# Transposes of attention weights, values and gate inputs moved from TensorE to the DMA engines as 16-bit planes

## The chip, the cores and the metric

The kernel runs on one core of a Trainium2 chip. A core has a matrix engine (TensorE, PE in the profile, with its weight loads as PEld), a vector engine (VectorE, DVE), an activation engine (ScalarE, ACT), a general engine (GpSimd, POOL) and a queue engine (SyncE, SP). Each runs its own list of instructions strictly in order and waits on semaphores; 16 DMA engines move data between the device memory and the on-chip memory (SBUF). TensorE writes to a second on-chip memory (PSUM). The metric is the device time in microseconds of one execution, as a median over runs.

## The reference, cut to what matters

One layer of an encoder is applied to 256 prompt positions and 64 sample positions (320 columns, `T`), model width 2048:

```python
xn = rmsnorm(x, norm_mix)
q, k, v, u, vs, g = split(xn @ w_in)
a  = stick_breaking(q, k, v)             # 8 heads of 128; the sample also sees 256 cached keys
u  = gelu(u);  vs = rmsnorm(gelu(vs), sgu_norm)
bb = spatial_gate(u, vs)                 # per group: s = w_spatial @ vs over 128 positions, then u * s
merged = g_a * (a @ w_branch_a) + g_b * (bb @ w_branch_b)
h = x + merged @ w_out
h = h + (silu(gate) * up) @ w_down       # gate, up = rmsnorm(h) @ w_gate_up
y = rmsnorm(h)
```

Everything is 32-bit floating point. The stick-breaking weights `w` of a head are a matrix of queries by keys. The step after it, `w @ v`, and the spatial gate both sum over positions, so TensorE needs positions on the partitions: the weights, the values `v` and the normalised `vs` have to be transposed on the way.

## The kernel before, in words

All activations are kept with features on the 128 partitions and the 320 positions along the row. Every dense product is made of blocks: `block()` (line 88 on) loads 1024 columns of weights (512 KB) with one DMA of SP into a buffer `raw` (3 buffers), ScalarE rounds them to `wh` (line 75), VectorE takes the remainder `wl = raw - wh` (line 76; 4 buffers of each), and TensorE does 8 x 3 products of 128 by 320 (lines 83, 84, 85). After each such block the counter `tick()` goes up by one; `at(tick, fn)` puts a piece of side work at a later tick. The blocks are numbered here from 0, from the first block after the first two heads; block 0 is the first of the `k` projection of head 2.

The order on each engine is fixed when the program is built: a scheduler places instructions by dependences and priorities, and DMAs wrapped in `keep_in_program_order` keep their mutual order. At run time an engine that waits holds everything that stands behind it.

Attention goes by pairs of heads, 0 to 3. `att_scores` makes scores `z`, ScalarE and VectorE turn them into weights (absolute value, exponential, logarithm, a running sum, exponential) in `z[0]` (128x640), `z[1]` (128x384 used) and `wown` (128x128). `att_turn` then transposes 14 blocks of 128x128 on TensorE with the identity matrix: 4 of `v` (line 383), 1 of `vo`, the sample's part of `v` which GpSimd collects (384), 6 of `z` (387), 2 of `z[0]` (389) and `wown` (390). The results lie in PSUM; ScalarE and VectorE copy them to `av` and `wt` (lines 393 to 397). `att_out` multiplies them (403) and splits the result into `B` (117, 118, 416, 417). In the spatial gate, `sgu_gain` scales `vs`, `sgu_turn` transposes 5 blocks for each of 4 pairs of groups (490, 491) and ScalarE copies them out (494, 495), and `sgu_mix` multiplies (503, 505).

Of the kernel before, what the change touches and what calls it, by code (L numbers as in the profile page):

```python
# [8 lines left out]
F32 = mybir.dt.float32  # L9
# [4 lines left out]
P = 128  # L14
TP = 256
TS = 64
T = TP + TS
D = 2048
KD = D // P
H = 8  # L20
# [13 lines left out]
def stream_step(ctx: ExitStack, tc: tile.TileContext, xT, w_in, w_a, w_b, w_out, w_gu, w_down,  # L34
                gains, ws_t, bs, ck_t, cv, y_t, k_t, v_t, sv_t):
    nc = tc.nc
# [65 lines left out]
    def pair(name):  # L102
        return big.tile([P, 2 * T], F32, tag="D", bufs=8, name=name)
# [36 lines left out]
    ident = const.tile([P, P], F32, name="ident")  # L140
# [142 lines left out]
    attn = {}  # L283
    att_ctx = ExitStack()
    apool = att_ctx.enter_context(tc.tile_pool(name="attn", bufs=1))
# [21 lines left out]
    Z, KT = 384, T + PAST  # L307
# [13 lines left out]
    def att_new(p):  # L321
        attn[p] = {"q": apool.tile([P, 2, T], F32, tag="q", bufs=2, name="q"),
                   "k": apool.tile([P, 2, KT], F32, tag="k", bufs=2, name="k"),
                   "v": apool.tile([P, 2, T], F32, tag="v", bufs=2, name="v"),
                   "vo": apool.tile([P, P], F32, tag="vo", name="vo")}

    def att_keys(p):
        tc.keep_in_program_order(nc.sync.dma_start(
# [44 lines left out]
        for r in ROWS:  # L373
            nc.scalar.activation(out=wown[r, r], in_=z[1][r, Z:], func=AF.Exp)

    def att_turn(p):

        s = attn[p]
        z, v = s["z"], s["v"]
        ba, bb, bs_, bv = aux(), aux(), aux(), aux()  # L380
        cols = lambda t, i: t[:, i * P : (i + 1) * P]
        for i in range(4):
            nc.tensor.transpose(cols(bv, i), v[:, i // 2, i % 2 * P : (i % 2 + 1) * P], ident)  # L383
        nc.tensor.transpose(cols(ba, 3), s["vo"], ident)
        for j, b in enumerate((ba, bb)):
            for i in range(3):
                nc.tensor.transpose(cols(b, i), cols(z[j], i), ident)  # L387
        for i in range(2):
            nc.tensor.transpose(cols(bs_, i), cols(z[0], 3 + i), ident)
        nc.tensor.transpose(cols(bs_, 2), wown, ident)  # L390
        wt = s["wt"] = apool.tile([P, 3 * Z], F32, tag="wt", name="wt")
        av = s["av"] = apool.tile([P, 5 * P], F32, tag="av", name="av")
        nc.scalar.copy(out=av[:, 0 : 4 * P], in_=bv)
        nc.vector.tensor_copy(wt[:, 0:Z], ba[:, 0:Z])
        nc.vector.tensor_copy(av[:, 4 * P :], ba[:, Z:])
        nc.scalar.copy(out=wt[:, Z : 2 * Z], in_=bb[:, 0:Z])
        nc.scalar.copy(out=wt[:, 2 * Z :], in_=bs_[:, 0:Z])

    def att_out(p):
        s = attn.pop(p)  # L400
        wt, av, cvt = s["wt"], s["av"], s["cv"]
        po = aux1(), aux()
        mm = lambda out, a, b, first, last: nc.tensor.matmul(out, a, b, start=first, stop=last, skip_group_check=True)  # L403

        mm(po[0][:, TP : TP + P], av[:, 4 * P :], wt[:, 2 * Z + 2 * P :], True, False)
        for j, r in enumerate(ROWS):
            for i in range(2):
                lo = 2 * Z + i * P + j * TS
                mm(po[0][:, TP + j * TS : TP + (j + 1) * TS], cvt[:, i, j, :], wt[:, lo : lo + TS], False, i == 1)
        for j in range(2):  # L410
            mm(po[j][:, 0:TP], av[:, 2 * j * P : (2 * j + 1) * P], wt[:, j * Z : j * Z + TP], True, False)
            mm(po[j][:, P:TP], av[:, (2 * j + 1) * P : (2 * j + 2) * P], wt[:, j * Z + TP : (j + 1) * Z], False, True)
# [8 lines left out]
    def head_out(name, ps, h):  # L421
        s = attn[h // 2]
        o = s[name][:, h % 2, 0:T]
        if name == "q":
            nc.vector.scalar_tensor_tensor(out=o, in0=ps, scalar=QSCALE, in1=got["rx"],
                                           op0=ALU.mult, op1=ALU.mult)
        else:
            nc.vector.tensor_tensor(out=o, in0=ps, in1=got["rx"], op=ALU.mult)
            nc.gpsimd.dma_start(out=(k_t if name == "k" else v_t)[h], in_=o)
        if name == "v":  # L430
            nc.gpsimd.tensor_copy(s["vo"][:, ROWS[h % 2]], o[:, TP:T])

    def first_out():
        for name, b in (("q", 0), ("k", 1), ("v", 2)):
# [33 lines left out]

    us, _ = halves(H, "us")
    bT: dict[int, tuple] = {}  # L470
    vown, vnat = {}, {}

    def sgu_norm():
        got["rv"] = rms("rv", [sq.total], H * P)
        sgu_gain(0)

    def sgu_gain(p):

        own = vown[p] = apool.tile([P, 2, T], F32, tag="q", bufs=2, name="vown")[:, 0, 0:P]
        for j in range(2):  # L480
            g = 2 * p + j
            for out, r in ((vs[g][:, 0:TP], slice(0, TP)), (own[:, j * TS : (j + 1) * TS], slice(TP, T))):
                nc.vector.scalar_tensor_tensor(out=out, in0=vs[g][:, r], scalar=g_sgu[:, g : g + 1],
                                               in1=got["rv"][:, r], op0=ALU.mult, op1=ALU.mult)
            nc.gpsimd.dma_start(out=sv_t[g], in_=own[:, j * TS : (j + 1) * TS])

    def sgu_turn(p):
        pt, po = aux(), aux()
        for i in range(4):
            nc.tensor.transpose(pt[:, i * P : (i + 1) * P], vs[2 * p + i // 2][:, i % 2 * P : (i % 2 + 1) * P], ident)  # L490
        nc.tensor.transpose(po[:, 0:P], vown.pop(p), ident)
        t = apool.tile([P, 5 * P], F32, tag="av", name="vsn") if p % 2 else apool.tile([P, 3 * Z], F32, tag="wt", name="vsn")
        vn = vnat[p] = t[:, 0 : 5 * P].rearrange("p (i d) -> p i d", i=5)
        nc.scalar.copy(out=vn[:, 0:4].rearrange("p i d -> p (i d)"), in_=pt)
        nc.scalar.copy(out=vn[:, 4], in_=po[:, 0:P])
        if p + 1 < H // 2:
            sgu_gain(p + 1)
# [20 lines left out]
    def sgu_both(p):  # L518
        if p:
            sgu_mix(p - 1)  # L520
        if p < H // 2:
            sgu_turn(p)
# [14 lines left out]
    for m in range(KD):  # L537
        gate = []
        for i in range(2):
            ps = block(w_in[5 * H + i * KD + m], xs)  # L540
            t = t320("ev")
# [8 lines left out]
        t = t320("mg", 1)  # L550
# [5 lines left out]
        lo = mpool.tile([P, T], F32R, tag="C", bufs=32, name="ml")  # L556
# [72 lines left out]
    ms, r = (const.tile([P, 3], F32, name=f"col{i}") for i in range(2))  # L629
# [9 lines left out]
    for n in (1, 1, 2, 2, 2, 2, 2, 2, 1, 1):  # L639
        y = ypair[done // 2].rearrange("p (c t) -> p c t", c=2)[:, done % 2 : done % 2 + n, :]  # L640
# [57 lines left out]
```

## Time and profile before

| | |
|---|---|
| Median of 3 runs | 1716.69 us (1716.69 to 1718.19) |
| The profiled execution | 1716.78 us |
| Its span, first to last instruction | 1715.0 us |
| TensorE busy | 1702.2 us, 99% |
| VectorE, ScalarE, GpSimd busy | 861.9, 658.8, 46.1 us |
| Mean rate of the DMA engines | 154 GB/s |
| Attention and spatial gate, from its first scores to the last mix | about 63 to 327 us |

A row of the page or of a view gives, for a group of instructions, the source line, the engine, the operation, what it writes and reads, the shape, the count, the busy time in us, the mean of one in ns, and the idle time of the engine just ahead of them with what ended it. A timeline row gives start, duration, engine, line. Matmuls overlap in the pipeline, so a matmul's duration is longer than the distance to the next one; the distance is what it costs.

### The profile page before, as it was taken

The numbers are of one execution on the slowest core, as the hardware profiler recorded it, in microseconds if no ns is written. First come the engines' busy times: TensorE is split into PE (matmuls) and PEld (weight loads), VectorE is DVE, ScalarE is ACT, GpSimd is POOL, SyncE is SP. The second block draws the span as 40 slices with busy tenths as digits, with TensorE's granted clock in tenths as the row PEclk, the third lists the DMA queues.
The fourth block names the chain that finished last, engine by engine and source line by source line (L and its number), as shares of the span: only waits on it lengthen the run. The fifth ranks groups of instructions, "written<-read, shape, count | busy, mean of one in ns | idle before, by whom it ended". The sixth has DMA issues, their size and how long they took to land.

```text
span 1715.0 us, 27450 instructions
## 1 busy us (share of the span) xinstructions
PE 1702.2 (99%) x11616; PEld 1696.7 (99%) x11616; DVE 861.9 (50%) x1097; ACT 658.8 (38%) x819; POOL 46.1 (3%) x73
## 2 busy tenths in 40 slices
PE   9999999999999999999999999999999999999997
PEld 9999999999999999999999999999999999999997
DVE  7655446544444445555444444444444444444454
ACT  6454454433333333444333332233333323333332
POOL 0100011000000000110000000000000000000000
PEclk9999999999999999999999999999999999999999
DMA  7554444444444445554444445444444444444453
GB/s 260 162 193 143 144 154 145 139 148 148 149 153 152 148 152 165 174 171 149 150 148 148 150 152 153 148 148 148 152 151 152 148 148 150 151 153 149 130 150 114
DMA packets 80331, 263.32 MB, mean 154 GB/s; under 512 B 9008, under 2 KB 15408, under 8 KB 80208
## 3 DMA queue, kind: packets, MB, share of 16 engines
q1 hardware_dynamic: 78704, 258.25, 46.6%
q0 software_dynamic: 1088, 3.02, 0.5%
q8 instruction: 91, 1.49, 0.3%
q10 hardware_dynamic: 416, 0.31, 0.1%
q14 instruction: 32, 0.26, 0.0%
HBM read 256.03 MB, written 5.51 MB: 152 GB/s over the span
## 4 chain that ended last, share of the span: by engine, by line
issue 54%; PE 45%; DVE 0%; DMA 0%; ACT 0%; POOL 0%; POOLq 0%; ACTq 0%; DVEq 0%
PE acc L83 13%; PE acc L84 13%; PE acc L85 13%; PE aux L219 2%; PE acc L219 1%; PE aux L403 1%; DVE h L637 0%; DMA raw<-w_in 0%; PE aux L505 0%; PE aux L343 0%; PE aux L345 0%; PE aux L387 0%; PE aux L342 0%; PE aux L490 0%; PE aux L383 0%
## 5 line engine op out<-in xcount | busy, mean ns | idle before, releaser
L75 ACT CAST wh<-raw 128x1024 fp32r<-128x1024 f32 x468 | 484.5, 1036 | 988.0 <-PE acc L84 796.3
L76 DVE TENSOR_TENSOR wl<-raw,wh 128x1024 fp32r<-128x1024 f32 x468 | 564.2, 1206 | 506.4 <-ACT wh L75 503.9
L83 PE MATMUL acc<-A,wh 128*128 128x320 f32 x2464 | 763.1, 310 | 0.0
L85 PE MATMUL acc<-A,wl 128*128 128x320 f32 x2464 | 761.5, 309 | 0.0
L84 PE MATMUL acc<-A,wh 128*128 128x320 f32 x2464 | 761.4, 309 | 0.0
L83 PEld LDWEIGHTS acc<-A,wh 128*128 128x128 f32 x2464 | 462.6, 188 | 2.1 <-issue 2.0
L84 PEld LDWEIGHTS acc<-A,wh 128*128 128x128 f32 x2464 | 462.6, 188 | 0.2
L85 PEld LDWEIGHTS acc<-A,wl 128*128 128x128 f32 x2464 | 462.6, 188 | 0.0
L85 PE MATMUL acc<-B,wl 128*128 128x320 f32 x960 | 296.6, 309 | 0.0
L83 PE MATMUL acc<-B,wh 128*128 128x320 f32 x960 | 296.6, 309 | 0.0
L84 PE MATMUL acc<-B,wh 128*128 128x320 f32 x960 | 296.6, 309 | 0.0
L83 PEld LDWEIGHTS acc<-B,wh 128*128 128x128 f32 x960 | 180.2, 188 | 0.0
L84 PEld LDWEIGHTS acc<-B,wh 128*128 128x128 f32 x960 | 180.2, 188 | 0.0
L85 PEld LDWEIGHTS acc<-B,wl 128*128 128x128 f32 x960 | 180.2, 188 | 0.0
L83 PE MATMUL acc<-mh,wh 128*128 128x320 f32 x256 | 79.1, 309 | 0.0
L84 PE MATMUL acc<-ml,wh 128*128 128x320 f32 x256 | 79.1, 309 | 0.0
L85 PE MATMUL acc<-mh,wl 128*128 128x320 f32 x256 | 79.1, 309 | 0.0
L597 DVE TENSOR_TENSOR bb<-acc,rh 128x320 f32<-128x320 f32 x44 | 21.6, 491 | 57.8 <-PE acc L85 57.8
L594 DVE TENSOR_TENSOR ev<-acc,rh 128x320 f32<-128x320 f32 x44 | 21.6, 491 | 56.4 <-PE acc L85 56.3
L83 PEld LDWEIGHTS acc<-mh,wh 128*128 128x128 f32 x256 | 48.0, 188 | 0.0
L84 PEld LDWEIGHTS acc<-ml,wh 128*128 128x128 f32 x256 | 48.0, 188 | 0.0
L85 PEld LDWEIGHTS acc<-mh,wl 128*128 128x128 f32 x256 | 48.0, 188 | 0.0
(173 smaller groups left out, 696.2 us busy)
## 6 DMA issues: line engine op xcount, KB each, us to landing
raw<-w_gu SPq DMA_DIRECT2D x176, 512.0 KB, 3.5
raw<-w_in SPq DMA_DIRECT2D x141, 512.0 KB, 3.6
raw<-w_down SPq DMA_DIRECT2D x80, 512.0 KB, 3.5
raw<-w_out SPq DMA_DIRECT2D x32, 512.0 KB, 3.6
raw<-w_a SPq DMA_DIRECT2D x16, 512.0 KB, 3.5
raw<-w_b SPq DMA_DIRECT2D x16, 512.0 KB, 3.5
raw<-w_down SPq DMA_DIRECT2D x16, 256.0 KB, 2.7
xr<-xT SPq DMA_DIRECT2D x16, 160.0 KB, 2.6
```

What stands on the lines that cost most here:

```text
L75: nc.scalar.copy(out=wh[:, : n * P], in_=raw[:, : n * P])
L76: nc.vector.tensor_tensor(out=wl[:, : n * P], in0=raw[:, : n * P], in1=wh[:, : n * P].bitcast(F32), op=ALU.subtract)
L83: nc.tensor.matmul(ps[:, :T], a, x[0], start=first, stop=False)
L84: nc.tensor.matmul(ps[:, :T], a, x[1], start=False, stop=False)
L85: nc.tensor.matmul(ps[:, :T], b, x[0], start=False, stop=last)
L219: nc.tensor.matmul(first[b][h][:, :T], w[:, (h * n + j) * P : (h * n + j + 1) * P], xs[c + j][i], start=not last and c + j + i == 0, stop= ...
L403: mm = lambda out, a, b, first, last: nc.tensor.matmul(out, a, b, start=first, stop=last, skip_group_check=True)
L594: nc.vector.tensor_tensor(out=t, in0=pg, in1=got["rh"], op=ALU.mult)
L597: nc.vector.tensor_tensor(out=u, in0=pu, in1=got["rh"], op=ALU.mult)
```

## The change

The 76 transposes on TensorE go. In their place `apart` has ScalarE copy a 32-bit tile into two planes of 16-bit halves, one behind the other in a row (read with a stride, written straight). `turn` has SP issue one DMA that transposes all 128x128 blocks of both planes (a 128x1280 tile of 16-bit words is 10 blocks, 320 KB; the `wp1` tile is 128x1024, 8 blocks, 256 KB). `together` has VectorE copy the two planes back into every second half-word of a 32-bit tile. The planes and the turned planes are 128x640 tiles of the pool with 8 buffers that also holds `z`, `vs` and `us`. For a pair of heads there are three DMA transposes (`vp`, `wp0`, `wp1`), for a pair of groups one (`vsp`): 16 in all. GpSimd's copy to `vo` goes. The ticks of the side work change: the output of a pair of heads comes 16 ticks after its start instead of 14.

```diff
+    def planes(name, n):
+        return pair(name)[:, 0:n].bitcast(U16).rearrange("p (w n) -> p w n", w=2)
+    def apart(to, src):
+        nc.scalar.copy(out=to, in_=src.bitcast(U16).rearrange("p (n w) -> p w n", w=2))
+    def turn(src):
+        to = planes("turned", src.shape[2])
+        flat = lambda t: t.rearrange("p w n -> p (w n)")
+        tc.keep_in_program_order(nc.sync.dma_start(
+            out=flat(to).rearrange("p (b r) -> p b r", r=P), in_=flat(src), transpose=True))
+        return to
+    def together(to, src):
+        nc.vector.tensor_copy(to.bitcast(U16).rearrange("p (n w) -> p w n", w=2), src)
...
+        y = s["wp"] = planes("wp0", 5 * P), planes("wp1", 4 * P)
+        apart(y[0], z[0])
+        apart(y[1][:, :, 0:Z], z[1][:, 0:Z])
+        apart(y[1][:, :, Z:], wown)
-    def att_turn(p):
...
-        for i in range(4):
-            nc.tensor.transpose(cols(bv, i), v[:, i // 2, i % 2 * P : (i % 2 + 1) * P], ident)
-        nc.tensor.transpose(cols(ba, 3), s["vo"], ident)
-        for j, b in enumerate((ba, bb)):
-            for i in range(3):
-                nc.tensor.transpose(cols(b, i), cols(z[j], i), ident)
-        for i in range(2):
-            nc.tensor.transpose(cols(bs_, i), cols(z[0], 3 + i), ident)
-        nc.tensor.transpose(cols(bs_, 2), wown, ident)
...
-        nc.scalar.copy(out=av[:, 0 : 4 * P], in_=bv)
-        nc.vector.tensor_copy(wt[:, 0:Z], ba[:, 0:Z])
-        nc.vector.tensor_copy(av[:, 4 * P :], ba[:, Z:])
-        nc.scalar.copy(out=wt[:, Z : 2 * Z], in_=bb[:, 0:Z])
-        nc.scalar.copy(out=wt[:, 2 * Z :], in_=bs_[:, 0:Z])
+    def att_turn(p, what):
         s = attn[p]
+        s[what] = [turn(t) for t in ((s["vp"],) if what == "vt" else s["wp"])]
+    def att_join(p, what):
...
+            together(av, t[0])
...
+            together(wt[:, 0 : 5 * P], t[0])
+            together(wt[:, 5 * P :], t[1])
...
         if name == "v":
-            nc.gpsimd.tensor_copy(s["vo"][:, ROWS[h % 2]], o[:, TP:T])
...
+            apart(s["vp"][:, :, j * TP : (j + 1) * TP], o[:, 0:TP])
+            apart(s["vp"][:, :, 4 * P + j * TS : 4 * P + (j + 1) * TS], o[:, TP:T])
...
         at(now + 2, att_scores, p)
-        at(now + 4, att_rows, p)
-        at(now + 10, att_turn, p)
-        at(now + 14, att_out, p)
+        at(now + 6, att_turn, p, "vt")
+        at(now + 11, att_rows, p)
+        at(now + 8, att_join, p, "vt")
+        at(now + 12, att_turn, p, "wt")
+        at(now + 14, att_join, p, "wt")
+        at(now + 16, att_out, p)
...
     def sgu_turn(p):
...
-        for i in range(4):
-            nc.tensor.transpose(pt[:, i * P : (i + 1) * P], vs[2 * p + i // 2][:, i % 2 * P : (i % 2 + 1) * P], ident)
-        nc.tensor.transpose(po[:, 0:P], vown.pop(p), ident)
...
-        nc.scalar.copy(out=vn[:, 0:4].rearrange("p i d -> p (i d)"), in_=pt)
-        nc.scalar.copy(out=vn[:, 4], in_=po[:, 0:P])
+        vturned[p] = turn(vplane.pop(p))
+    def sgu_join(p):
...
+        together(t[:, 0 : 5 * P], vturned.pop(p))
...
-    for p in range(H // 2 + 1):
-        at(base + 4 * p + 2 + (p == 0), sgu_both, p)
+    for p, mix in enumerate((9, 11, 14, 18)):
+        at(base + 1 + 3 * p, sgu_gain, p)
+        at(base + 6 + 3 * p, sgu_turn, p)
+        at(base + (8, 10, 13, 16)[p], sgu_join, p)
+        at(base + mix, sgu_mix, p)
```

More of the change, by code (lines that the diff above doesn't have):

```diff
@@ L323, in att_new @@
                    "k": apool.tile([P, 2, KT], F32, tag="k", bufs=2, name="k"),
-                   "v": apool.tile([P, 2, T], F32, tag="v", bufs=2, name="v"),
-                   "vo": apool.tile([P, P], F32, tag="vo", name="vo")}
+                   "v": apool.tile([P, 2, T], F32, tag="v", bufs=2, name="v")}
+    U16 = mybir.dt.uint16
+    def planes(name, n):
[10 more added lines that the diff above has]
+        nc.vector.tensor_copy(to.bitcast(U16).rearrange("p (n w) -> p w n", w=2), src)
     def att_keys(p):
@@ L374, in att_scores @@
             nc.scalar.activation(out=wown[r, r], in_=z[1][r, Z:], func=AF.Exp)
-    def att_turn(p):
-        s = attn[p]
-        z, v = s["z"], s["v"]
-        ba, bb, bs_, bv = aux(), aux(), aux(), aux()
-        cols = lambda t, i: t[:, i * P : (i + 1) * P]
-        for i in range(4):
-            nc.tensor.transpose(cols(bv, i), v[:, i // 2, i % 2 * P : (i % 2 + 1) * P], ident)
-        nc.tensor.transpose(cols(ba, 3), s["vo"], ident)
-        for j, b in enumerate((ba, bb)):
-            for i in range(3):
-                nc.tensor.transpose(cols(b, i), cols(z[j], i), ident)
-        for i in range(2):
[L389 to L394, printed above, removed]
-        nc.vector.tensor_copy(av[:, 4 * P :], ba[:, Z:])
-        nc.scalar.copy(out=wt[:, Z : 2 * Z], in_=bb[:, 0:Z])
-        nc.scalar.copy(out=wt[:, 2 * Z :], in_=bs_[:, 0:Z])
+        y = s["wp"] = planes("wp0", 5 * P), planes("wp1", 4 * P)
[3 more added lines that the diff above has]
+    def att_turn(p, what):
+        s = attn[p]
+        s[what] = [turn(t) for t in ((s["vp"],) if what == "vt" else s["wp"])]
+    def att_join(p, what):
+        s = attn[p]
+        t = s[what]
+        if what == "vt":
+            av = s["av"] = apool.tile([P, 5 * P], F32, tag="av", name="av")
+            together(av, t[0])
+        else:
+            wt = s["wt"] = apool.tile([P, 9 * P], F32, tag="wt", name="wt")
+            together(wt[:, 0 : 5 * P], t[0])
+            together(wt[:, 5 * P :], t[1])
     def att_out(p):
@@ L403, in att_out @@
         mm = lambda out, a, b, first, last: nc.tensor.matmul(out, a, b, start=first, stop=last, skip_group_check=True)
-        mm(po[0][:, TP : TP + P], av[:, 4 * P :], wt[:, 2 * Z + 2 * P :], True, False)
+        mm(po[0][:, TP : TP + P], av[:, 4 * P :], wt[:, 8 * P :], True, False)
         for j, r in enumerate(ROWS):
             for i in range(2):
-                lo = 2 * Z + i * P + j * TS
+                lo = Z + i * P + j * TS
                 mm(po[0][:, TP + j * TS : TP + (j + 1) * TS], cvt[:, i, j, :], wt[:, lo : lo + TS], False, i == 1)
         for j in range(2):
-            mm(po[j][:, 0:TP], av[:, 2 * j * P : (2 * j + 1) * P], wt[:, j * Z : j * Z + TP], True, False)
-            mm(po[j][:, P:TP], av[:, (2 * j + 1) * P : (2 * j + 2) * P], wt[:, j * Z + TP : (j + 1) * Z], False, True)
+            w = wt[:, j * 5 * P : j * 5 * P + Z]
+            mm(po[j][:, 0:TP], av[:, 2 * j * P : (2 * j + 1) * P], w[:, 0:TP], True, False)
+            mm(po[j][:, P:TP], av[:, (2 * j + 1) * P : (2 * j + 2) * P], w[:, TP:], False, True)
         aT[2 * p] = split("B", po[0][:, 0:T])
@@ L430, in head_out @@
         if name == "v":
-            nc.gpsimd.tensor_copy(s["vo"][:, ROWS[h % 2]], o[:, TP:T])
+            j = h % 2
+            if j == 0:
+                s["vp"] = planes("vp", 5 * P)
+            apart(s["vp"][:, :, j * TP : (j + 1) * TP], o[:, 0:TP])
+            apart(s["vp"][:, :, 4 * P + j * TS : 4 * P + (j + 1) * TS], o[:, TP:T])
     def first_out():
@@ L470, in stream_step @@
     bT: dict[int, tuple] = {}
-    vown, vnat = {}, {}
+    vplane, vturned, vnat = {}, {}, {}
     def sgu_norm():
         got["rv"] = rms("rv", [sq.total], H * P)
-        sgu_gain(0)
     def sgu_gain(p):
-        own = vown[p] = apool.tile([P, 2, T], F32, tag="q", bufs=2, name="vown")[:, 0, 0:P]
+        own = apool.tile([P, 2, T], F32, tag="q", bufs=2, name="vown")[:, 0, 0:P]
         for j in range(2):
@@ L485, in sgu_gain @@
             nc.gpsimd.dma_start(out=sv_t[g], in_=own[:, j * TS : (j + 1) * TS])
+        y = vplane[p] = planes("vsp", 5 * P)
+        for j in range(2):
+            apart(y[:, :, j * TP : (j + 1) * TP], vs[2 * p + j][:, 0:TP])
+        apart(y[:, :, 4 * P :], own)
     def sgu_turn(p):
-        pt, po = aux(), aux()
-        for i in range(4):
[L490 to L493, printed above, removed]
-        nc.scalar.copy(out=vn[:, 0:4].rearrange("p i d -> p (i d)"), in_=pt)
-        nc.scalar.copy(out=vn[:, 4], in_=po[:, 0:P])
-        if p + 1 < H // 2:
-            sgu_gain(p + 1)
+        vturned[p] = turn(vplane.pop(p))
+    def sgu_join(p):
+        t = apool.tile([P, 5 * P], F32, tag="av", name="vsn") if p % 2 else apool.tile([P, 9 * P], F32, tag="wt", name="vsn")
+        together(t[:, 0 : 5 * P], vturned.pop(p))
+        vnat[p] = t[:, 0 : 5 * P].rearrange("p (i d) -> p i d", i=5)
     def sgu_mix(p):
@@ L516, in sgu_mix @@
             bT[g] = split("B", b)
[L518 to L522, printed above, removed]
     base = state["tick"]
     at(base + 1, sgu_norm)
-    for p in range(H // 2 + 1):
-        at(base + 4 * p + 2 + (p == 0), sgu_both, p)
+    for p, mix in enumerate((9, 11, 14, 18)):
[3 more added lines that the diff above has]
+        at(base + mix, sgu_mix, p)
     for g in range(H):
```

## The prediction

> **What bounds the kernel now.** I read the page first: busy times, then TensorE's row in the 40 slices and the granted clock.
>
> ```profile
> PE 1702.2 (99%) x11616; PEld 1696.7 (99%) x11616; DVE 861.9 (50%) x1097; ACT 658.8 (38%) x819; POOL 46.1 (3%) x73
> PE   9999999999999999999999999999999999999997
> PEclk9999999999999999999999999999999999999999
> ```
>
> TensorE works in every slice at full clock; the others are half idle. So what leaves TensorE shortens the time, as long as nothing makes TensorE wait. Who waits for whom is the second view, the grouped instructions with the idle time ahead of them:
>
> ```profile
> L75 ACT CAST wh<-raw 128x1024 fp32r<-128x1024 f32 x452 | 474.5, 1050 | 973.1 <-PE acc L84 781.4 <-issue 161.1 <-DMA raw<-w_in 17.9
> L76 DVE TENSOR_TENSOR wl<-raw,wh 128x1024 fp32r<-128x1024 f32 x452 | 553.2, 1225 | 506.3 <-ACT wh L75 503.9 <-PE acc L219 2.3
> ```
>
> ScalarE's rounding waits for TensorE (781 us in all), that is for a free `wh` buffer. The weights run ahead. How far, the third view tells, the timeline, here of VectorE and TensorE at block 8:
>
> ```profile
> 77.90 3.49 DVE L76 TENSOR_TENSOR wl<-raw,wh 128x1024 fp32r<-128x1024 f32 x3
> 78.66 0.31 PE L83 MATMUL acc<-A,wh 128*128 128x320 f32 x1
> 78.80 0.31 PE L84 MATMUL acc<-A,wh 128*128 128x320 f32 x1
> 79.39 0.31 PE L85 MATMUL acc<-A,wl 128*128 128x320 f32 x1
> ```
>
> Five products from 78.66 to 79.39 are 0.147 us apart, so a block of 24 takes 3.52 us. In steady running a `wl` is ready some 8 us before it is used (4 buffers: three blocks, 10.6 us, less 1.05 and 1.22 for rounding and remainder). But each `att_scores` takes ScalarE and VectorE for some 12 us, and the lead shrinks: the first of the three remainders in that row, block 8's, ends at 79.1 and is used at 79.39.
>
> **The change part by part.** *Transposes removed.* The chain of work that ended last gives TensorE's pace in them, the groups their count.
>
> ```profile
> 135.22 0.66 PE aux L387 x6
> 311.32 0.44 PE aux L490 x4
> ```
> ```profile
> L387 PE MATMUL aux<-ident,z 128*128 128x128 f32 x24 | 3.3, 272 | 0.0
> L490 PE MATMUL aux<-ident,vs 128*128 128x128 f32 x16 | 2.6, 272 | 0.0
> L383 PE MATMUL aux<-ident,v 128*128 128x128 f32 x16 | 2.4, 272 | 0.0
> L389 PE MATMUL aux<-ident,z 128*128 128x128 f32 x8 | 1.5, 272 | 0.0
> L491 PE MATMUL aux<-ident,vown 128*128 128x128 f32 x4 | 1.1, 273 | 0.0
> L384 PE MATMUL aux<-ident,vo 128*128 128x128 f32 x4 | 1.1, 273 | 0.0
> L390 PE MATMUL aux<-ident,wown 128*128 128x128 f32 x4 | 1.1, 272 | 0.0
> ```
>
> 24+16+16+8+4+4+4 = 76 transposes, each 272 ns long but 0.66/6 = 0.11 us apart: 8.3 us on the path. All other products stay. This is the whole gain there can be: -8.3 us.
>
> *ScalarE.*
>
> ```profile
> L75 ACT CAST wh<-raw 128x512 fp32r<-128x512 f32 x16 | 9.9, 622 | 14.9 <-PE acc L84 14.9
> L393 ACT COPY av<-aux 128x512 f32<-128x512 f32 x4 | 2.3, 578 | 0.0
> L397 ACT COPY wt<-aux 128x384 f32<-128x384 f32 x4 | 2.0, 492 | 0.0
> ```
>
> Its price per column comes from its casts of 1024 and of 512: (1050-622)/512 = 0.84 ns, plus 194 ns. For a pair of heads: `v` 2 x (0.62+0.30), `z[0]` 1.26 (1280 half-words), `z[1]` 0.84, `wown` 0.41, together 4.4 us; away go 0.58 and two of 0.49. A pair of groups gets 1.65 us, and loses a 0.59 and a short one. In all it is about +14 us.
>
> ```profile
> core 0: us, PE busy (x) PEld busy (x) DVE busy (x) ACT busy (x) POOL busy (x), PEclk, DMA share, GB/s
> 60.00:252.00 192.00, 192.00 (x1320) 188.06 (x1319) 103.06 (x156) 97.78 (x137) 16.22 (x24) 1.00 0.48 157
> ```
>
> In the attention alone ScalarE is idle for 94 us and VectorE for 89. Where they matter is order: the 2.5 us of `wp0` and `wp1` stand ahead of roundings 11, 20 and 32, just where the lead is thin. At 11 ScalarE waits for a DMA anyway (3 us); at 20 and 32 they cost 1 to 2 us of lead.
>
> *VectorE.* A join writes 1280 or 1024 half-words with a stride. The nearest rows are its copies from PSUM:
>
> ```profile
> L394 DVE COPY wt<-aux 128x384 f32<-128x384 f32 x4 | 2.2, 550 | 0.0
> L350 DVE COPY z<-aux 128x128 f32<-128x128 f32 x8 | 2.2, 279 | 0.0
> ```
>
> At (550-279)/256 = 1.06 ns per column a join takes 1.5 or 1.2 us, perhaps half; 16 joins, 23 us, against 3.3 us of copies that go. I take 1.5. VectorE has the room, but in its list the joins stand between remainders: the `v` join ahead of blocks 12, 22, 33 and 44, the `wt` joins ahead of 13 and 14, of 23 (both), of 35 (both), of 50 and 51. **A join waits for a DMA, and behind it wait the remainders that TensorE needs.** That is the one dangerous place. GpSimd's eight copies to `vo`, off the path, go.
>
> *SP and the DMA queues.* 16 transposing DMAs, and the one of `cv` is moved. No row shows a transposing DMA. What is near:
>
> ```profile
> raw<-w_in SPq DMA_DIRECT2D x141, 512.0 KB, 3.6
> y_t<-h SPq DMA_DIRECT2D x6, 320.0 KB, 2.3
> k<-ck_t SPq DMA_DIRECT2D x4, 256.0 KB, 4.6
> sv_t<-vown POOLq DMA_DIRECT2D x8, 32.0 KB, 2.0
> ```
>
> The lower end is a copy at the rate that the queues reach in a burst, some 250 GB/s: 1.3 us of queue time for 320 KB. The upper end is the slowest row with lines of 256 bytes, like those of a 128x128 block of half-words: 32 KB in 2.0 us, ten blocks one after the other, 20 us. I take 2 us of queue time and about 5 us to landing, near the rows of 320 and 256 KB. The Trainium skill (DMA: Bandwidth & Descriptors, section on latency and other measured facts) gives 261 GB/s for a transposing DMA; by it 320 KB are 1.3 us, no stall arises below, and the sum would be 1708.5 us. No run here shows it yet.
>
> *What this does to the lead.* Two stretches after scores (the last two columns are the DMA engines' share and GB/s), then SP, ScalarE and TensorE in the second of them:
>
> ```profile
> 79.10:90.20 11.10, 11.10 (x78) 11.10 (x77) 6.67 (x8) 3.98 (x5) 1.06 (x2) 1.00 0.78 267
> 117.70:127.60 9.90, 9.90 (x69) 9.90 (x68) 5.27 (x6) 2.41 (x3) 0.54 (x1) 1.00 0.78 249
> ```
> ```profile
> 117.69 1.60 SPq L70 DMA_DIRECT2D raw<-w_in  x2
> 120.06 10.26 SPq L70 DMA_DIRECT2D raw<-w_in  x4
> ```
> ```profile
> 127.65 1.05 ACT L75 CAST wh<-raw 128x1024 fp32r<-128x1024 f32 x1 [1.48 <-PE acc L85]
> ```
> ```profile
> 139.85 0.31 PE L85 MATMUL acc<-A,wl 128*128 128x320 f32 x1
> ```
>
> There three loads go out almost at once, as the `raw` buffers were held, and the DMA engines are at 78%. Into that burst SP's new list puts, for pair 1: load 21, `vp`, load 22, `cv`, the keys, load 23, `wp0`, `wp1`. Load 23, landed by 127.6 before, and then both transposes carry 896 KB + 256 KB more. At 249 GB/s that is 4.7 us; the burst starts 1.1 us sooner (the `B` splits of pair 0 no longer stand in it), so `wp1` lands at about 131.2. Joins and remainder 23 end at 134.2. The use is at 139.85 less pair 1's own 14 transposes, 1.5 us: 138.3. Margin 4 us. For pair 2:
>
> ```profile
> 169.34 16.28 SPq L70 DMA_DIRECT2D raw<-w_in  x6
> 188.24 0.31 PE L85 MATMUL acc<-A,wl 128*128 128x320 f32 x1
> ```
>
> Pair 2 has the same order. There `wp0`, `wp1` and the splits push rounding 32, so load 35 goes out at about 172.8 instead of 169.3, the transposes land near 179.5, and joins and remainder 35 end at 183.4; it is used at 188.3-1.5 = 186.8. Margin 3 us. Pair 0:
>
> ```profile
> 88.72 1.22 DVE L76 TENSOR_TENSOR wl<-raw,wh 128x1024 fp32r<-128x1024 f32 x1
> ```
> ```profile
> 98.51 0.31 PE L85 MATMUL acc<-A,wl 128*128 128x320 f32 x1
> ```
>
> Pair 0 is tighter. Remainder 13 ends at 89.9 and is used at 98.5-1.5 = 97.0; 4.4 us of transfers and 1.5 of a join leave 1 to 1.5 us. Pair 3's `wp0` comes behind load 51, out of the burst, and the gate's four behind loads 61, 63, 67 and 71. By the same reckoning both have some 7 us to spare beyond a landing in 5 us. At my 2 us per 320 KB the three bursts get 1.9 us more than at the copy rate: pair 0 stalls by 0.5, the others not. I add 0.7 for what SP loses in issuing. Sum: 1716.78 - 8.3 + 1.2 = 1709.7 us for the profiled execution (span 1715.0, 1.8 outside it), which lies 0.1 above the median.
>
> **The rivals.** *Slower transposes.* The mechanism is the join that holds VectorE. With queue time r times a copy's, a burst takes (r-1) x 3.7 us more; what exceeds margins of 1.3, 4 and 3 is stall. At r = 2.5 that is 4.3+1.6+2.6 = 8.5 us: from there the kernel is slower. At r = 4: 9.8+7.1+8.1 = 25, 1733 us. For it: small lines (the 32 KB row runs at 16 GB/s). Against: 256 KB beside loads in 4.6 us. *About even.* r from 2.2 to 2.8, stalls of 5 to 11 us: 1713 to 1720. *Block after block.* Ten blocks at 2.0 us each: 28 blocks in a burst take 56 us, three bursts stall by about 50 each, pair 3 by 20, the gate by 40: about 1920. Only a fixed price per block would do it, and that 2.0 us is mostly one latency, so I hold it unlikely. The Trainium skill (VectorE: DVE Perf Modes, section on the three transpose paths) has 1309 ns for one 128x128 block by DMA against 390 on TensorE; multiplied by ten, its figure is an estimate of 1815 us on the same reckoning. *The change does not do what it says:* only if TensorE did not go straight on to the next block; its row has no gap, so I give that nothing.
>
> **How the numbers follow.** Forecast 0.57 (stall below 5 us, 1708.5 to 1713), even 0.12, slower transposes 0.23, block after block 0.08. A difference under 0.2%, 3.4 us, can't be told from none. Faster: 0.57; same 0.12; slower 0.31. The likeliest own range is 1708 to 1713; the range for all is 1707.5 (the whole gain and a little of the runs' scatter) to 1733 (r = 4), with about 0.1 above it.
>
> **What would show it.** Right: no transposes on TensorE, 8.3 us fewer in the chain, DMA rows of `turned` landing within 5 us, TensorE waiting for `wl` by 2 us at most, near blocks 12 to 14. Wrong: VectorE's joins (line 344) waiting for `turned` for many us, TensorE's products waiting for `wl`, first at blocks 13, 23 and 35; or ScalarE late at 8.

## The result and the profile after

The changed kernel takes 1709.15 us (median of 4 runs, 1708.48 to 1710.02); the kernel before, on the same chip, 1717.44 us. The ratio is 0.9948, 95% interval 0.9936 to 0.996: faster by 8.3 us. In the profiled execution (1708.48 us) the span is 1706.7 us, 8.3 less than the 1715.0 before.

The page of the changed kernel, busy times and the DMA queue that SP and ScalarE use:

```profile
PE 1693.9 (99%) x11540; PEld 1688.5 (99%) x11540; DVE 870.2 (51%) x1105; ACT 670.0 (39%) x838; POOL 42.2 (2%) x65
q1 hardware_dynamic: 98672, 263.23, 48.7%
```

TensorE is busy for 8.3 us less (1702.2 before) with 76 instructions fewer. Apart from GpSimd, which lost its copies (46.1 to 42.2 us), everything else grew: VectorE by 8.3 us, ScalarE by 11.2, the DMA queue from 46.6% of 1715.0 us to 48.7% of 1706.7. None of it shows in the time, as the view of TensorE's waits says (columns: us in total, times, longest):

```profile
PE aux L190 <- POOL ones L143: 1.2, 1, 1.2
PE acc L219 <- ACT wh L209: 1.0, 1, 1.0
PE aux L657 <- POOL col L653: 0.2, 1, 0.2
```

The first two are at the start and the third at the end; the kernel before has the same three. Not once does TensorE wait for a remainder (`wl`).

The new operations: joins (line 344) and planes (line 334) as grouped instructions of single shapes, then the DMA issues (count, median us to landing), then the time for which each issue held SP's queue (min/median/max in ns):

```profile
L344 DVE COPY av<-turned 128x1280 uint16<-128x1280 uint16 x4 | 3.6, 907 | 8.5 <-DMA turned<-vp 8.5
L344 DVE COPY wt<-turned 128x1280 uint16<-128x1280 uint16 x4 | 3.6, 906 | 10.1 <-DMA turned<-wp 10.1
L344 DVE COPY vsn<-turned 128x1280 uint16<-128x1280 uint16 x4 | 3.6, 906 | 5.9 <-DMA turned<-vsp 5.7
L344 DVE COPY wt<-turned 128x1024 uint16<-128x1024 uint16 x4 | 3.0, 753 | 1.8 <-DMA turned<-wp 1.8
L334 ACT COPY wp<-z 128x1280 uint16<-128x1280 uint16 x4 | 5.0, 1261 | 0.1
```
```profile
turned<-wp SPq DMA_TRANSPOSE x8, 6.6
turned<-vp SPq DMA_TRANSPOSE x4, 5.2
turned<-vsp SPq DMA_TRANSPOSE x4, 5.1
```
```profile
L339 SPq DMA_TRANSPOSE turned<-wp x8: 1557/2876/3544, 85.0 to 229.4; - x8
L339 SPq DMA_TRANSPOSE turned<-vp x4: 1263/1487/2054, 80.7 to 210.3; - x4
```

VectorE does wait at its joins for the DMAs, 26 us in all (8.5 + 10.1 + 5.7 + 1.8), with remainders behind it: what the prediction called the one dangerous place is there, but it is covered. The last view is a surprise: a weight load's issue usually holds SP for 0.33 us, a transposing one for 1.3 to 3.5. How the loads are pushed back by it is seen in SP's timeline of pair 1 (the row at 122.01 is `wp0` and `wp1`; load 24 waits for it until 128.32):

```profile
117.60 1.27 SPq L339 DMA_TRANSPOSE turned<-vp  x1
121.63 0.33 SPq L70 DMA_DIRECT2D raw<-w_in  x1
122.01 6.21 SPq L339 DMA_TRANSPOSE turned<-wp  x2
128.32 1.00 SPq L70 DMA_DIRECT2D raw<-w_in  x2
```

And what it does to the leads of the remainders 13, 23 and 35, the prediction's three places: when VectorE makes them, and when TensorE first uses them:

```profile
92.28 1.21 DVE L76 TENSOR_TENSOR wl<-raw,wh 128x1024 fp32r<-128x1024 f32 x1
132.87 1.21 DVE L76 TENSOR_TENSOR wl<-raw,wh 128x1024 fp32r<-128x1024 f32 x1
177.94 1.22 DVE L76 TENSOR_TENSOR wl<-raw,wh 128x1024 fp32r<-128x1024 f32 x1
```
```profile
97.00 0.31 PE L85 MATMUL acc<-A,wl 128*128 128x320 f32 x1
136.82 0.31 PE L85 MATMUL acc<-A,wl 128*128 128x320 f32 x1
183.69 0.31 PE L85 MATMUL acc<-A,wl 128*128 128x320 f32 x1
```

The leads are 3.5, 2.7 and 4.5 us. The same reckoning over blocks 12 to 51 finds the least at block 18, 2.0 us; block 8's 0.3 us is as before, ahead of the change.

**A yardstick for the experiments.** The first product of a weight block (line 83) starts 48.7 to 52.1 us after the span's start, differently from run to run, though all kernels here do the same until then. So I also compare the stretch from the first to the last product of line 83 on `A`, which holds all that the change touches. It comes from that group's row, after the durations; in the kernel before and after:

```profile
L83 PE MATMUL acc<-A,wh x2464: 303/309/551, 48.7 to 1615.3; 128*128 128x320 f32 x190
```
```profile
L83 PE MATMUL acc<-A,wh x2464: 302/309/551, 48.8 to 1607.0; 128*128 128x320 f32 x190
```

That is 1566.6 us before and 1558.2 after, 8.4 less (each number is rounded to 0.1). The stretch is that of one execution, the traced one. For three kernels below (half as much transposing again, plain copies, transposes issued from ScalarE) that one was the shortest of the kernel's runs: 1713.29, 1710.73 and 1722.81 us, where the medians are 1715.83, 1712.70 and 1726.00. For these the ratios put the cost higher than the stretch does.

### The profile page after: what moved, and what is told of

Read it like the earlier page. It is cut to its first block, busy times and chain, and to the rows that moved or that the text cites. A ratio compares the mean times of both kernels' runs of the same rounds, so it can differ in the third digit from the quotient of the medians.

```text
span 1706.7 us, 27337 instructions
## 1 busy us (share of the span) xinstructions
PE 1693.9 (99%) x11540; PEld 1688.5 (99%) x11540; DVE 870.2 (51%) x1105; ACT 670.0 (39%) x838; POOL 42.2 (2%) x65
## 3 DMA queue, kind: packets, MB, share of 16 engines
q1 hardware_dynamic: 98672, 263.23, 48.7%
## 4 chain that ended last, share of the span: by engine, by line
issue 54%; PE 44%; DVE 0%; DMA 0%; ACT 0%; POOL 0%; POOLq 0%; ACTq 0%; DVEq 0%
PE acc L83 14%; PE acc L84 13%; PE acc L85 13%; PE aux L219 2%; PE acc L219 1%; PE aux L421 1%; DVE h L659 0%; DMA raw<-w_in 0%; PE aux L530 0%; PE aux L362 0%; PE aux L364 0%; PE aux L361 0%; POOL sq_h L175 0%; PE aux L155 0%; PE aux L657 0%
```

## The experiments

My theory: TensorE's pace sets the end, so the gain is its 76 transposes at 0.11 us, and the new work costs nothing as long as it stays inside the leads. Rivals: that part of the gain came from the other edits (later ticks, no copies out of PSUM), or that the new work costs something that a larger gain covers.

### The two parts alone

The attention as changed, the gate as before (and the reverse in the second kernel):

```diff
-    def sgu_join(p):
-        together(t[:, 0 : 5 * P], vturned.pop(p))
+            nc.tensor.transpose(pt[:, i * P : (i + 1) * P], vs[2 * p + i // 2][:, i % 2 * P : (i % 2 + 1) * P], ident)
+        nc.tensor.transpose(po[:, 0:P], vown.pop(p), ident)
...
+        nc.scalar.copy(out=vn[:, 0:4].rearrange("p i d -> p (i d)"), in_=pt)
+        nc.scalar.copy(out=vn[:, 4], in_=po[:, 0:P])
```

> The attention's part of the change alone (56 of the 76 TensorE transposes gone; the spatial gate is as in the kernel before). Theory (the gain is TensorE's removed transposes at 0.11 us each, and everything else lies in reserves): 56 x 0.11 = 6.1 us under the kernel before, a ratio of 0.9964. Rival A (the eight large transposing DMAs and the joins of the attention cost part of it, the gate's do not): a gain of 3 to 5 us, with TensorE waiting on remainders (wl) in the attention's blocks. Rival B (part of the gain comes from the later turns and the freed copies, not from TensorE): more than 7 us.

> The gate's part of the change alone (20 of the 76 TensorE transposes gone; the attention is as in the kernel before). Theory: 20 x 0.11 = 2.2 us under the kernel before, a ratio of 0.9987; together with the run that has the attention's part alone the gains add up to the whole change's 8.3 us. Rival A (the parts disturb each other, or one of them costs): the two gains do not add up to 8.3 within 1.5 us. Rival B (the gate's wait of TensorE for its transposes' copies was part of the time before): 4 us or more.

Measured: the attention alone 0.9966 of the time before (0.9952 to 0.9979), the gate alone 0.9988 (0.9979 to 0.9997). The rows of line 83, attention alone, then gate alone:

```profile
L83 PE MATMUL acc<-A,wh x2464: 302/309/551, 51.2 to 1611.6; 128*128 128x320 f32 x190
```
```profile
L83 PE MATMUL acc<-A,wh x2464: 302/309/551, 50.7 to 1615.1; 128*128 128x320 f32 x190
```

The stretches are 1560.4 and 1564.4 us, 6.2 and 2.2 under the kernel before, where 56 and 20 transposes give 6.1 and 2.2. The parts add up to the whole; neither rival shows.

### The transposes put back, unread

```diff
+    def idle_transposes(n):
+        for k in range(0, n, 4):
+            t = aux()
+            for i in range(min(4, n - k)):
+                nc.tensor.transpose(t[:, i * P : (i + 1) * P], ident, ident)
...
+        idle_transposes(5 if what == "vt" else 9)
```

> The changed kernel with 76 TensorE transposes put back that nothing reads (128x128 of the identity into accumulators, 5, 9 and 5 at the places where the turns are issued); the transposing DMAs, the planes and the joins stay. Theory: TensorE's path grows by 76 x 0.11 = 8.3 us, so the time is that of the kernel before within 1 us. Rival A (the DMA transposes or the joins cost something that the gain covers): over 1 us slower than the kernel before. Rival B (the later turns, the missing evacuations of PSUM or the idle GpSimd gave part of the gain): 2 us or more faster than the kernel before.

Measured: ratio 1.0 (0.9992 to 1.0009). The row of line 83:

```profile
L83 PE MATMUL acc<-A,wh x2464: 302/309/551, 49.1 to 1615.7; 128*128 128x320 f32 x190
```

1566.6 us, that of the kernel before to the tenth. So planes, transposing DMAs, joins and later ticks together cost and gain nothing here: all of the 8.3 us is TensorE's. This settles the cause of the gain.

### More transposing: how much reserve there was

Half as much again, then twice as much; the third kernel issues the same additional bytes as plain copies:

```diff
+        for w in range(2):
+            more = apool.tile([P, 5 * P], U16, tag="more", bufs=3, name="more")[:, 0 : src.shape[2]]
+            tc.keep_in_program_order(nc.sync.dma_start(
+                out=more.rearrange("p (b r) -> p b r", r=P), in_=src[:, w], transpose=True))
```

(`range(1)` for half as much again; `out=more, in_=src[:, w]` for the plain copies.)

> The changed kernel with half as much transposing again: behind each transposing DMA a second one of one plane (the low half-words, 160 KB or 128 KB) into a buffer that nobody reads. Theory (SyncE's queue is held per transposing DMA, 1.3 to 3.5 us each in the changed kernel, and later weight loads and remainders eat a lead that is 2.0 to 4.5 us at blocks 12 to 24): the two extra at a pair's weights hold the queue about 3 us more, the thinnest leads (blocks 18, 22, 23) go to 0 to 1 us, and TensorE stalls 0 to 2 us in all: 1709 to 1711. Rival A (there is no reserve, each extra hold costs its length): 16 DMAs of 0.8 to 1.8 us, 1724 to 1730. Rival B (the reserve is far larger than the leads, as loads catch up): no stall, and the leads as they were.

> The changed kernel with twice the transposing: behind each transposing DMA two more, one of each plane, into buffers that nobody reads (three buffers, so that the last of four at a pair's weights may wait for the first to land). Theory: at a pair's weights SyncE's queue is held some 12 us in place of 6, against leads of 2.0 to 4.5 us behind it at blocks 12 to 24; TensorE stalls 2 to 5 us at pairs 1 and 2 and less at the others, 1713 to 1722, on remainders or main parts whose loads were issued late. Rival A (every hold on the path): 1735 or more. Rival B (reserve far larger): 1709 to 1710.

> As the kernel with twice the transposing (two more DMAs behind each, into buffers that nobody reads), but the additional 32 DMAs are plain copies of the same bytes from SBUF to SBUF, not transposes. Tells apart what the additional DMAs cost there (14.3 us from the first product of a weight block on). Theory (the hold of SyncE's queue belongs to the transposing form, 1.2 us or more per DMA against 0.3 to 0.5 of a plain one): 0 to 3 us more than the changed kernel. Rival A (it is the bytes on the DMA engines, or the number of DMAs between weight loads): 8 us or more, as with the transposes.

Measured, as ratios to the kernel before: 0.9984 (0.9975 to 0.9994), 1.0038 (1.0023 to 1.0053) and 0.9967 (0.9954 to 0.998). The rows of line 83, of the kernel with half more, twice, and plain:

```profile
L83 PE MATMUL acc<-A,wh x2464: 302/309/551, 48.7 to 1611.8; 128*128 128x320 f32 x190
```
```profile
L83 PE MATMUL acc<-A,wh x2464: 302/309/551, 51.5 to 1624.1; 128*128 128x320 f32 x190
```
```profile
L83 PE MATMUL acc<-A,wh x2464: 302/309/551, 49.3 to 1609.3; 128*128 128x320 f32 x190
```

Against the changed kernel's 1558.2 the stretch is 4.9, 14.4 and 1.8 us longer. TensorE's waits in the kernel with half more, and in that with twice as much:

```profile
PE acc L85 <- DVE wl L76: 3.2, 4, 1.7
```
```profile
PE acc L85 <- DVE wl L76: 5.5, 4, 3.4
PE acc L83 <- ACT wh L75: 5.2, 3, 2.7
```

Three things follow. First, the changed kernel stands near the edge: half as much again takes back more than half of the gain, twice as much all of it. Second, my expectations for both were too low (1709 to 1711 us and 1713 to 1722; the medians are 1715.83 and 1725.37). For half more I had set the hold against each block's own lead, but VectorE's list carries a delay on. Its timeline in that kernel (lines 383 to 393 are the softmax):

```profile
115.44 2.08 DVE L390 TENSOR_TENSOR_SCAN e<-ones,e 128x128 f32<-128x128 f32 x5
119.73 2.35 DVE L76 TENSOR_TENSOR wl<-raw,wh 128x1024 fp32r<-128x1024 f32 x2
```

The same work in the changed kernel:

```profile
111.69 2.08 DVE L386 TENSOR_TENSOR_SCAN e<-ones,e 128x128 f32<-128x128 f32 x5
115.98 2.35 DVE L76 TENSOR_TENSOR wl<-raw,wh 128x1024 fp32r<-128x1024 f32 x2
```

All of it is 3.75 us later, while TensorE was on time until then. The loads that were held back at pair 0 delayed remainders 16 and 17 (101.16 and 103.78 in the changed kernel, 105.07 and 107.53 here), behind them VectorE took the next pair's scores out of PSUM late, and remainder 18, which stands behind the softmax, came 1.7 us too late for TensorE. Third, it is the transposing form that costs: the same bytes as plain copies cost 1.8 us in place of 14.4. What differs in SP's rows is the hold, for `more<-wp` as transposes and as plain copies:

```profile
L343 SPq DMA_TRANSPOSE more<-wp x16: 1210/1274/3714, 92.3 to 255.0; - x16
```
```profile
L343 SPq DMA_DIRECT2D more<-wp x16: 464/590/932, 88.0 to 236.5; - x16
```

That the hold alone makes the difference isn't shown, because the transposes also keep the DMA queue busy for longer: 0.521 x 1723.7 = 898 us with them and 0.516 x 1708.9 = 882 us with the plain copies, against 0.487 x 1706.7 = 831 in the changed kernel. The queue's load alone doesn't explain it, though: the plain copies add 51 of those 67 us and cost 1.8 us of time, not 14.4.

### What the hold goes by

Each transposing DMA split in two, one per plane; and the whole ones issued from ScalarE:

```diff
-        tc.keep_in_program_order(nc.sync.dma_start(
-            out=flat(to).rearrange("p (b r) -> p b r", r=P), in_=flat(src), transpose=True))
+        for w in range(2):
+            tc.keep_in_program_order(nc.sync.dma_start(
+                out=to[:, w].rearrange("p (b r) -> p b r", r=P), in_=src[:, w], transpose=True))
```
```diff
-        tc.keep_in_program_order(nc.sync.dma_start(
+        tc.keep_in_program_order(nc.scalar.dma_start(
```

> The changed kernel with each transposing DMA split in two, one per plane (32 in place of 16, the same bytes). Theory: the same time as the changed kernel, within 0.5 us from the first product of a weight block on. It tells what the hold of SyncE's queue goes by: if by bytes or blocks, two halves hold it together as long as the whole (1.3 to 3.5 us); if by the DMA, about twice as long, and the leads at blocks 18 to 24 shrink by 1.3 to 3 us to 0 or a little more.

> The changed kernel with the 16 transposing DMAs issued from ScalarE in place of SyncE. Theory: the hold goes with the issuing engine: SyncE's weight loads are no longer late (leads of the remainders at blocks 13 to 24 back at the 3 to 10 us of the kernel before), but each issue holds ScalarE 1.3 to 3.5 us, and with it the main parts (wh) of the weights, whose lead is about one remainder (1.2 us) and a wait longer than that of the remainders; no stall or one under 1 us: 1709 to 1710. Rival A (ScalarE's hold stops main parts and TensorE): 1713 or more. Rival B (the hold is not of the issuing engine but of the DMA queue's depth): ScalarE is held under 0.5 us an issue and SyncE's loads stay late.

Measured: split 0.9951 (0.9934 to 0.9967), its stretch 1558.3 us, that of the changed kernel. From ScalarE 1.0036 (1.0023 to 1.0049); in its traced execution the stretch is 11.1 us longer than that of the changed kernel, and the other four runs took 0.8 to 4.3 us more than that one. The split kernel's holds:

```profile
L340 SPq DMA_TRANSPOSE turned<-wp x16: 1210/1326/2424, 87.4 to 233.5; - x16
L340 SPq DMA_TRANSPOSE turned<-vp x8: 1211/1295/1342, 82.8 to 213.6; - x8
L340 SPq DMA_TRANSPOSE turned<-vsp x8: 1211/1288/1372, 267.8 to 305.0; - x8
```

Half the bytes are held nearly as long: 1.21 us at least, against 1.26 for the whole. So there is a floor per DMA, and `vp` and `vsp` in two cost 1.7 times as much (two of 1.3 us in place of 1.5, by the medians); only the large holds of `wp`, 2.9 us in the middle, don't grow (two of 1.3), so those are mostly something else, perhaps a wait behind the DMA just issued. The remainders at blocks 18 and 23 led by only 0.6 and 0.2 us there, and still no time was lost: a lead is worth nothing until it is used up.

From ScalarE the forecast failed, and rival A was right in its time but not in its reason. Main parts were not what TensorE waited for; its waits, and VectorE's row ahead of the worst of them:

```profile
PE acc L85 <- DVE wl L76: 7.5, 3, 4.6
PE aux L528 <- DVE vsn L344: 1.1, 1, 1.1
```
```profile
99.54 0.88 DVE L344 COPY av<-turned 128x1280 uint16<-128x1280 uint16 x1 [8.96 <-DMA turned<-vp]
100.31 1.21 DVE L76 TENSOR_TENSOR wl<-raw,wh 128x1024 fp32r<-128x1024 f32 x1
```

VectorE stood for 9 us at the join of `v` (its DMA was issued at 83.33 and released the join 16 us later), and the remainder behind it came 4.6 us late. This is the prediction's dangerous place, reached by a late DMA. It wasn't the transpose alone that was late. ScalarE's roundings at 94.34 and 100.59 waited 5.0 and 5.2 us for their weights, the first of them here:

```profile
94.34 1.05 ACT L75 CAST wh<-raw 128x1024 fp32r<-128x1024 f32 x1 [5.02 <-DMA raw<-w_in]
```

From 90.0 to 96.6 us the DMA engines moved 108 GB/s here, and in the changed kernel 260 to 313 from 84.0 to 96.6, although they were not idle here (their share was 1.22; it adds up the packets' times, which can overlap). So with the transposes in a second queue, beside SP's loads, all transfers were slow at this place; why they were stays open. The hold itself did go with the issuing engine, 1.3 to 4.3 us of ScalarE's queue:

```profile
L339 ACTq DMA_TRANSPOSE turned<-wp x8: 1269/2225/4321, 100.6 to 243.1; - x8
```

It does not stop ScalarE's work altogether: during the first hold, that of `vp` from 83.33 to 85.79, at least three of its copies began.

### The joins

On GpSimd in place of VectorE; and, in another kernel, done twice by VectorE:

```diff
-        nc.vector.tensor_copy(to.bitcast(U16).rearrange("p (n w) -> p w n", w=2), src)
+        nc.gpsimd.tensor_copy(to.bitcast(U16).rearrange("p (n w) -> p w n", w=2), src)
```
```diff
+        for _ in range(2):
             nc.vector.tensor_copy(to.bitcast(U16).rearrange("p (n w) -> p w n", w=2), src)
```

> The changed kernel with the 16 joins on GpSimd instead of VectorE, so that no remainder (wl) stands behind a join that waits for a DMA. Theory (the waits of VectorE at the joins, 26 us in the trace of the changed kernel, are all inside the remainders' lead of 2.0 us or more): the time of the changed kernel, 1709.2 within 0.7 us, while the lead of the remainders at blocks 18 and 23 grows to that of the kernel before (3.1 and 9.9 us) unless the late loads set it. Rival A (VectorE's hold costs): 1 to 3 us faster than the changed kernel. Rival B (GpSimd is slow at the join and the attention's products wait for it): slower than the changed kernel by 2 us or more.

> The changed kernel with each of the 16 joins done twice by VectorE, so that a join costs 1.8 or 1.5 us in all (0.91 and 0.75 in the changed kernel), about what the prediction took. Theory (at that price the remainders still have their lead: blocks 13, 18, 23 had 3.5, 2.0 and 2.8 us and lose 0.9 to 1.7 each): no stall, or one under 0.5 us at the thinnest; from the first product of a weight block on the same time as the changed kernel within 0.5 us. Rival (the prediction's reckoning of bursts was right and only the price of a join was too high): a stall at pair 0, blocks 13 and 14, of 0.5 us or more. The run with half as much transposing again has shown that a delay early in a pair is carried down VectorE's list to block 18, so 0.5 us there is possible for either.

Measured: 0.9956 both (0.9943 to 0.9968 and 0.994 to 0.9972), and the stretches are 1558.2 and 1558.3 us. Both kernels' first products came 2.1 and 2.6 us later in the span than the changed kernel's, which accounts for the times of the traced executions, 1710.59 and 1711.18 us against 1708.48. So neither moving the joins off VectorE nor doubling them changes the time. With the joins gone from VectorE the lead at block 23 grew from 2.7 to 5.1 us, not to the 9.9 of the kernel before: of the 7.2 us lost there, some 2.4 was VectorE's hold, 3.1 is TensorE coming earlier (28 transposes), and the rest, 1.7, may be the later loads; no run separates it. At block 18 it fell from 2.0 to 1.4, which stays open. With the joins doubled, blocks 13 and 14 kept 3.8 and 3.9 us: no stall at pair 0, at the price of a join that the prediction had taken.

## Why the prediction was right, and where its steps were off

Forecast 1709.7 us, measured 1709.15, inside the likeliest range. That they agree to 0.5 us is in part luck: the gain was forecast as 7.1 us and is 8.3, and the kernel before took 0.75 us more beside the changed kernel (1717.44) than in the runs that the forecast started from (1716.69). The mechanism was right: TensorE loses its transposes and waits for none of the new work. The two terms added to that, 0.5 and 0.7 us, were worth nothing. By its steps:

- *Transposes removed, -8.3 us, and nothing else to gain.* Right, shown by the unread transposes and by the two parts.
- *Pair 0 stalls by 0.5.* Wrong, and with it the margin of "1 to 1.5 us": it was 3.5. Remainder 13 was to end up to 5.9 us later than before; it ended 3.6 later (93.5 against 89.9). The doubled joins show that the price of the join was not the reason. The term that was too large is the 4.4 us of transfers: the step set the whole burst ahead of remainder 13, but only the joins of `vp` and `wp0` stand there, and VectorE waited 2.2 and 1.4 us for their DMAs (`wp1`'s join comes at 93.85, behind the remainder):

```profile
87.64 0.91 DVE L344 COPY av<-turned 128x1280 uint16<-128x1280 uint16 x1 [2.21 <-DMA turned<-vp]
91.48 0.91 DVE L344 COPY wt<-turned 128x1280 uint16<-128x1280 uint16 x1 [1.44 <-DMA turned<-wp]
```

- *0.7 us for what SP loses in issuing.* Mis-sized both ways: SP loses far more (1.3 to 3.5 us an issue), the time nothing. The prediction costed these issues as if they were ordinary ones. Of what the runs separate, this and not the queue's load is the likelier reason why doubled transposes made the kernel slower, as the plain copies show.
- *Pair 1: remainder 23 ends at 134.2, used at 138.3.* It ended at 134.1 and was used at 136.8. The end was right, by two errors that cancel: the join of `wp1` starts at 131.82, 0.6 us behind the landing that was forecast, and takes 0.4 us less. The use was wrong, because only pair 1's own 14 transposes were taken off and not the 14 of pair 0 before them (28 x 0.11 = 3.1 from 139.85). A gain made early brings every later use forward, and shortens each later lead. *Pair 2* had the same slip (42 transposes: 188.24 to 183.69), while load 35 went out earlier than forecast, and the margin was 4.5 instead of 3.
- *Joins of 1.5 and 1.2 us.* Measured 0.91 and 0.75, so 13.9 us in all (12 x 0.907 + 4 x 0.753) and not 23; the slope is (907-753)/256 = 0.60 ns per half-word against 1.06 for the copies from PSUM. The Trainium skill (VectorE: DVE Perf Modes, Mode 2×_2P) has copies within SBUF at two elements a cycle and PSUM sources excluded from it; the two slopes, a factor of 1.8 apart, agree roughly. The reading "perhaps half" was nearer than the value taken.
- *ScalarE's planes.* 1.26 us forecast for 1280 half-words, 1261 ns measured; +14 us in all, measured +11.2.
- *2 us of queue time per 320 KB.* The queue's time grew by 0.487 x 1706.7 - 0.466 x 1715.0 = 32 us, 2.0 us for each of the 16. Right, though to no better than 0.1, as the shares are rounded, and not as a price of bytes: with each DMA split in two the same bytes took 0.511 x 1708.8 - 0.466 x 1715.0 = 74 us more than before. The Trainium skill's 261 GB/s for a transposing DMA (DMA: Bandwidth & Descriptors, section on latency and other measured facts) is above what is seen here: 4.98 MB more in 32 us are 156 GB/s; the measurement decides. (The prediction's sum by that figure, 1708.5 us, also left out the 0.7 for SP.) *About 5 us to landing*: 5.1 to 6.6.
- *The rivals.* Block after block is excluded by those landings; the figure of 1309 ns for one block, from the Trainium skill (VectorE: DVE Perf Modes, section on the three transpose paths), does not multiply by ten. "Slower transposes" is a real cliff: with the transposing doubled the kernel does become slower than before, by stalls of TensorE on what VectorE and ScalarE make. Its formula gives 15 us for a doubled queue time (r = 2 x 2.0/1.3 = 3.1: 6.5 + 3.8 + 4.8), and 14.4 was measured, but that is luck: in that kernel the queue's time grew by 0.521 x 1723.7 - 0.466 x 1715.0 = 99 us over the kernel before, three times the 32 of the changed kernel, for which (r = 99/16/1.3 = 4.8) the formula gives over 30 us.
- *A sign of being wrong that came true.* VectorE's joins did wait for `turned` for many us, 26 in twelve waits, and still TensorE waited for no remainder. The sign to name was the lead of the remainders, not the wait.

## What to carry to other kernels

Where one engine is busy for 99% without a wait, an instruction taken from it is worth its distance to the next, here 0.11 us and not the 0.27 of its duration, and work moved to other engines is free until it uses up the smallest lead on the way back. That reserve is tested by doubling the new work, not by looking at busy shares: here twice the transposing turned 8 us gained into 6 lost, while VectorE, ScalarE and the DMA queue were about half busy or less (50%, 39% and 52%). Price a DMA in the list that issues it as well as in the queue, and follow a delay down the whole list of an in-order engine.

## What was not expected of the hardware

A transposing DMA holds the queue that issues it for 1.21 to 1.27 us at the least, whether it moves 160 or 320 KB, and for up to 3.5 us in the changed kernel; a weight load of 512 KB holds it for 0.33 when the queue is free.

A stall of TensorE costs more than the length that the view of waits gives. In the kernel with half as much transposing again four waits of 3.2 us in all made the stretch 4.9 us longer, and three other kernels show the same sign. TensorE's timeline at the longest of the four tells where most of the rest lies:

```profile
118.99 0.31 PE L84 MATMUL acc<-A,wh 128*128 128x320 f32 x1
121.01 0.42 PE L85 MATMUL acc<-A,wl 128*128 128x320 f32 x1 [1.71 <-DVE wl L76]
121.26 0.31 PE L83 MATMUL acc<-A,wh 128*128 128x320 f32 x1
```

The wait is counted from the end of the product ahead, 0.31 us after its start, but without a wait the next product would start after 0.147: 0.16 us is left out. And the next one follows the late product after 0.25 us, not 0.147. That makes 0.26 us a wait, 1.1 for the four; a fifth gap, too short for the view, adds some 0.4.

After a long stall the granted clock can fall too. The kernel with transposes from ScalarE, in stretches before, during and after its wait of 4.6 us (the eighth figure, before the DMA share and GB/s, is the clock):

```profile
90.00:96.60 6.60, 6.60 (x47) 6.60 (x46) 0.58 (x1) 1.05 (x1) 0.00 (x0) 1.00 1.22 108
96.60:101.50 4.90, 0.38 (x3) 0.12 (x1) 1.96 (x3) 0.91 (x1) 0.00 (x0) 0.96 0.83 278
101.50:104.40 2.90, 2.82 (x10) 2.82 (x11) 1.56 (x3) 0.14 (x1) 0.52 (x1) 0.50 1.11 133
```

For 2.9 us TensorE ran at half the clock, with 10 products where 20 would fit; from 104.4 on the clock is 0.99 again. The kernel with twice the transposing shows the same once, behind a wait of 2.7 us (197.9 to 200.9) and one of 0.7 close after it:

```profile
202.20:205.70 3.50, 3.50 (x14) 3.50 (x15) 3.10 (x4) 1.62 (x2) 0.00 (x0) 0.52 0.62 166
```

Behind its longest wait, 3.4 us, its products kept their pace. So in these two kernels the length of a single wait does not decide alone. The Trainium skill (TensorE: Matmul & The Clock Gate, Part 1) lets the clock halve after an idle window of about 3.4 us and come back after as long a busy one; the 4.6 us wait agrees, while the fall behind 2.7 and 0.7 us shows that the wait itself need not last 3.4.

Put together, the waits behind the first product, 0.26 us for each of them and the time lost at half the clock (2.9 us less 10 products at 0.147, and 3.5 less 14, both 1.4) come to 8.6 + 1.0 + 1.4 = 11.0 us for the transposes from ScalarE, where 11.1 was measured, and to 11.0 + 2.1 + 1.4 = 14.5 for twice the transposing, where it was 14.4. The prediction took a stall as the time by which an operand is late; that holds the 0.16 us, but neither the slow restart nor the clock, so its slower rivals were, if anything, too cheap.
